# A transformer block on one core: tiles 0 to 3 of the stage between attention and MLP made one sequence

## The chip, the core and the metric

The kernel runs on one NeuronCore of a Trainium2 chip. The core's engines work from instruction queues of their own: TensorE (PE, with its weight loads as PEld), VectorE (DVE), ScalarE (ACT), GpSimd (POOL), and SyncE (SP), which here only issues DMAs. The metric is the device time of one execution in microseconds; lower is better.

## What is computed

One block for a sequence of 1024 rows of width 1024, in float32. The reference, cut to what matters:

```python
def _hybrid_mixer(h, ...):            # two attentions side by side, 8 heads of 64 each
    ...
    return o @ w_out                  # o: [1024, 1024]

def _memory_xattn(h, mem, ...):       # 4 heads of 128 over a memory of 256 rows
    q = _rms_norm((h @ w_xq).reshape(B, L, 4, 128), xq_norm_g)
    ...
    s = jnp.einsum('bqhd,bmhd->bhqm', q, k) * 128 ** -0.5
    p = jax.nn.softmax(s, axis=-1)
    o = jnp.einsum('bhqm,bmhd->bqhd', p, v)
    return o.reshape(B, L, 512) @ w_xo

def _sq_relu_mlp(h, w_ff_in, w_ff_out):
    return jnp.square(jax.nn.relu(h @ w_ff_in)) @ w_ff_out

x = x + _hybrid_mixer(_rms_norm(x, norm1_g), ...)
x = x + _memory_xattn(_rms_norm(x, norm2_g), mem, ...)
x = x + _sq_relu_mlp(_rms_norm(x, norm3_g), w_ff_in, w_ff_out)
```

## The kernel before

The 1024 rows are eight tiles of 128. The program has a head (norm and input projections), a long middle part, and a tail (tiles 4 to 7 through what is left). In the middle part two streams of Python generators are woven into one program by `together` (L122): `attend`, the two attentions tile by tile, and `fill` (L1548), everything that comes after attention for tiles whose attention is done. `fill` yields an amount of work after each step, or a pair (tile, pace): it goes on when attention has finished that tile, and then gets its share of the program according to the pace. The framework's scheduler then puts the instructions of each engine in order with a timeline of its own, inserts the semaphores, and hands out buffers from rings. So the program's order is a priority, and what stands on an engine in the end has to be read from the instruction order.

Names in the profile: psS, psPT and psPV are attention's PSUM banks (scores, transposes, values). psD (two banks) and psM (one) belong to `fill`. `oT_dr` (`o` in the profile) is attention's output, written to DRAM by `finish` (L845 and L846: `oc`, then `o`). `finish` and the queries' loads (L696, `qin`) go over the SP queue like all of `fill`'s weights.

The stage around the change is `between` (L1055), called for tiles 0 and 1 and then for tiles 2 and 3. For each pair it does the following.

- Output projection of the first tile. The tile's `o` is loaded into the buffer `xl`, its rows of x into a ring of four residual buffers `b` (tag `b4`). `gemm` (L385) goes over four chunks of 256 columns of w_out; each chunk comes in four DMAs of 256 KB, into two rings of four buffers that are called `whi` and `wlo` here for their names elsewhere (`load_whole`, L310). w_out is read whole for every tile. In the profile these matmuls are `psD<-wlo,xl` and `psD<-whi,xl`; each chunk is added to the residual rows by DVE (L1048).
- Once attention has finished the second tile: its projection, in turns with the norm of the first tile (`norm_T2`, L353: square and sum on ACT, power on POOL, scaling on DVE, four transposes at a time on PE as `psM<-c_ident,relu`, copies to `xh`). Then the norm of the second tile.
- The memory attention of both tiles: w_xq (`psD<-wlo,xh`), for each tile and half of the heads the items of `memory_item` (L1150: norm of the query, transposes, scores as `psD<-h`, softmax), and when all four items are made, `memory_values` (L1185: transposes of the probabilities, L1194, then values, again `psD<-h`). The result goes to a `b` buffer.
- Output projection of the memory attention with w_xo (`psD<-wlo,b`, `psD<-whi,b`), added to the residual rows.

The residual rows of tiles 0 and 1 are then stored to DRAM (L1227). For the second pair the w_xo projection runs in turns with `pre_norms` (L1229), which loads tile 0's rows again (L1235) and tile 1's in halves (L1241, into the weight ring `wraw`) and makes the MLP's norms of these two tiles. `mlp` (L1255) loads tile 1's rows once more (L1260), makes the norms of tiles 2 and 3 and runs the MLP of all four tiles, interleaved with attention's later tiles.

## Time and profile before

| what | value |
|---|---|
| time, median of 3 runs (lowest, highest) | 1674.51 us (1671.83, 1677.1) |
| the profiled execution: time, span of its instructions | 1675.6 us, 1673.7 us |
| mean granted TensorE clock | 0.995 |
| first matmul of tile 0's output projection | 377.58 us |
| the MLP's first matmul | 613.5 us |
| DMA | 223.88 MB, mean 134 GB/s |

The span runs from the first to the last instruction of one profiled execution. An engine is busy while one of its compute instructions runs. Idle time is given with the instruction that it precedes, and with the one whose end released it. The granted clock is the share of full speed that PE was given. Attention and `fill` share PE from 378 us to the MLP; the MLP's stage runs from 613 us to its last stores at 1143 us.

### The profile page before, as it was taken

Reading aid. Unit: us, or ns where it says so; the run is one execution under the profiler, and the core shown is the slowest. Engines: PE = TensorE matmul, PEld = TensorE weight load, DVE = VectorE, ACT = ScalarE, POOL = GpSimd, SP = SyncE. Lnnn points to the kernel's source line nnn. Section 1 sums busy time; section 2 is a strip of 40 time slices with the busy share of each in tenths; the row PEclk is TensorE's granted clock in tenths of the full one; section 3 lists DMA queues with packets and bytes.
Section 4 is the critical chain, followed back from the end, with each engine's and each line's share of the span. In section 5 each row is a group of like instructions: output and inputs, shape, how many; then the busy total and the mean of one; then the engine's idle time right before and its main releaser. Section 6 shows DMA issues by size and latency. Waiting matters only on the chain.

```text
span 1673.7 us, 28995 instructions
## 1 busy us (share of the span) xinstructions
PE 1603.5 (96%) x9554; PEld 1410.7 (84%) x9554; DVE 1122.1 (67%) x2587; ACT 1112.0 (66%) x2783; POOL 960.2 (57%) x1110
## 2 busy tenths in 40 slices
PE   7998998989999889999999999999998999999998
PEld 6998997868788778888888888888888997878787
DVE  5476778776866874575565665556668657887875
ACT  5455898895698779956898559983555554444443
POOL 2265577574632547677666767672246854555466
PEclk9999999999999999999999999999999999999999
DMA  8875534348366322222222212254267452323254
GB/s 273 297 260 164 160 110 133 121 125 280 107 195 207 98 67 73 70 70 71 70 77 67 77 59 83 68 178 134 87 219 257 148 150 89 104 90 102 96 167 148
DMA packets 185447, 223.88 MB, mean 134 GB/s; under 512 B 24785, under 2 KB 138321, under 8 KB 185297
## 3 DMA queue, kind: packets, MB, share of 16 engines
q1 hardware_dynamic: 177360, 211.53, 39.6%
q0 software_dynamic: 7936, 10.49, 2.4%
q8 instruction: 76, 1.25, 0.3%
q14 instruction: 75, 0.61, 0.1%
HBM read 188.68 MB, written 33.29 MB: 133 GB/s over the span
## 4 chain that ended last, share of the span: by engine, by line
PE 64%; DVE 12%; DMA 8%; ACT 6%; POOL 5%; issue 4%; SPq 1%; ACTq 0%; POOLq 0%; DVEq 0%
PE psD L234 32%; PE psS L234 11%; PE psM L234 6%; PE psPT L234 4%; PE psPV L234 4%; PE psPT L832 4%; DVE wlo L268 2%; POOL wlo L268 2%; DMA wraw<-in_w_in_dram 2%; DVE S L815 1%; DVE pl L255 1%; DMA wraw<-in_w_ff_out_dram 1%; ACT dmask L776 1%; POOL S L822 1%; ACT whi L263 1%
## 5 line engine op out<-in xcount | busy, mean ns | idle before, releaser
L268 POOL TENSOR_TENSOR wlo<-wraw,whi 128x512 fp32r<-128x512 f32 (+1 forms) x228 | 317.0, 1396 | 197.3 <-ACT whi L263 194.6
L263 ACT ACTIVATE whi<-wraw 128x512 fp32r<-128x512 f32 x329 | 201.0, 626 | 174.2 <-DMA wraw<-in_w_ff_in_dram 30.6
L255 DVE TENSOR_TENSOR pl<-psPT,ph 128x512 fp32r<-128x512 f32 (+1 forms) x232 | 142.5, 621 | 73.9 <-ACT ph L254 72.6
L817 ACT ACTIVATE S<-S,mn 128x128 f32<-128x128 f32 (+7 forms) x192 | 143.1, 746 | 58.5 <-DVE mn L815 57.9
L234 PE MATMUL psD<-whi,h 128*128 128x512 f32 x512 | 175.8, 398 | 1.6 <-POOL h L1364 0.7
L822 POOL TENSOR_SCALAR S<-S,sums,gi 128x640 f32<-128x640 f32 (+7 forms) x128 | 111.5, 880 | 104.7 <-DVE sums L820 87.5
L254 ACT ACTIVATE ph<-psPT 128x512 fp32r<-128x512 f32 (+1 forms) x232 | 122.7, 541 | 49.7 <-PE psPT L832 42.0
L832 PE MATMUL psPT<-c_ident,S 128*128 128x128 f32 x816 | 132.5, 274 | 6.2 <-POOL S L822 4.0
L234 PE MATMUL psD<-wlo,xh 128*128 128x256 f32 (+1 forms) x512 | 131.3, 310 | 1.5 <-POOL wlo L268 0.8
L234 PE MATMUL psD<-whi,xh 128*128 128x256 f32 (+1 forms) x512 | 129.9, 312 | 2.7 <-DMA whi<-W 1.9
L268 DVE TENSOR_TENSOR wlo<-wraw,whi 128x512 fp32r<-128x512 f32 (+2 forms) x101 | 97.7, 975 | 51.0 <-ACT whi L263 48.1
L234 PE MATMUL psD<-whi,xl 128*128 128x256 f32 (+1 forms) x432 | 120.4, 315 | 0.2
L234 PE MATMUL psS<-K,qh 128*128 128x384 f32 (+3 forms) x288 | 106.7, 374 | 6.7 <-DVE mn L815 5.5
L832 PEld LDWEIGHTS psPT<-c_ident,S 128*128 128x128 f32 x816 | 97.6, 140 | 17.4 <-POOL S L822 7.7
L234 PEld LDWEIGHTS psD<-whi,h 128*128 128x128 f32 x512 | 95.6, 188 | 19.7 <-DVE b L1048 1.8
L234 PE MATMUL psD<-xh,whi 128*128 128x512 f32 (+1 forms) x296 | 102.7, 347 | 0.0
L234 PE MATMUL psD<-xh,wlo 128*128 128x512 f32 (+1 forms) x296 | 102.0, 345 | 0.0
L234 PE MATMUL psD<-xl,whi 128*128 128x512 f32 (+1 forms) x296 | 102.0, 346 | 0.0
L234 PE MATMUL psD<-wlo,h 128*128 128x512 f32 x256 | 101.3, 397 | 0.3 <-POOL wlo L268 0.3
L234 PEld LDWEIGHTS psD<-whi,xh 128*128 128x128 f32 x512 | 91.8, 191 | 7.4 <-issue 1.6
L234 PE MATMUL psS<-K,ql 128*128 128x384 f32 (+3 forms) x288 | 96.3, 338 | 0.4 <-DVE ql L255 0.4
L234 PEld LDWEIGHTS psD<-wlo,xh 128*128 128x128 f32 x512 | 91.6, 191 | 5.3 <-POOL wlo L268 1.2
(406 smaller groups left out, 5112.6 us busy)
## 6 DMA issues: line engine op xcount, KB each, us to landing
wraw<-in_w_ff_in_dram SPq DMA_DIRECT2D x44, 512.0 KB, 3.8
wraw<-in_w_ff_in_dram SPq DMA_DIRECT2D x64, 256.0 KB, 2.7
wraw<-in_w_ff_out_dram SPq DMA_DIRECT2D x64, 256.0 KB, 2.6
wraw<-in_w_ff_out_dram SPq DMA_DIRECT2D x24, 512.0 KB, 4.6
w<-in_w_ff_out_dram SPq DMA_DIRECT2D x20, 512.0 KB, 5.9
wlo<-in_w_out_dram SPq DMA_DIRECT2D x36, 256.0 KB, 5.1
whi<-in_w_out_dram SPq DMA_DIRECT2D x36, 256.0 KB, 5.1
wraw<-in_w_in_dram SPq DMA_DIRECT2D x24, 256.0 KB, 5.2
```

What stands on the lines that cost most here:

```text
L234: te.matmul(o, a, b, start=start, stop=stop)
L254: late["round"] = s.activation(hi, src, AF.Copy).ins
L255: late["split"] = v.tensor_tensor(lo, src, hi, op=ALU.subtract).ins
L263: s.activation(hi, raw, AF.Copy)
L268: (v if l == "v" else g).tensor_tensor(lo, raw, hi, op=ALU.subtract)
L776: s.activation(mask, src, AF.Sign, bias=c, accum_out=over)
L815: v.tensor_tensor_reduce(out=dst, in0=sp, in1=m, scale=1.0, scalar=mn[:, 0:1] if i else 3e38, op0=ALU.add, op1=ALU.min, accum_out=low)
L817: s.activation(S, S, AF.Exp, bias=low, scale=-1.0, accum_out=sums[:, hh:hh + 1])
L822: g.tensor_scalar(Ss[hh], Ss[hh], sums[:, hh:hh + 1], 1.0 if gate is None else gate[:, hh:hh + 1], op0=ALU.mult, op1=ALU.mult)
L832: te.transpose(p2[:, j, hh, :], S[:, (c + j) * P:(c + j + 1) * P], ident)
```

## The change

The two calls of `between` for tiles 0 to 3 become one generator, `four_tiles`. In its program order:

- Projection of tile 0; after attention's tile 1, the projection of tile 1 in turns with tile 0's norm; tile 1's norm; the first pair's memory scores and values.
- After attention's tile 2: **tile 2's output projection**, and only then the first pair's w_xo projection. Before, w_xo came first.
- After attention's tile 3: tile 3's projection in turns with tile 2's norm, tile 3's norm, the second pair's memory attention, and its w_xo projection in turns with the MLP's norms of tiles 0 and 1.

All four tiles' residual rows stay in the four `b` buffers until the MLP. The two stores and the reloads are gone, and the norm of tile 1 is an ordinary one. One buffer `xl` of four rows' width (`room`) holds two tiles' `o` in turns, the first pair's memory result and the norm's gain, which is loaded once instead of twice. The second pair's memory result lies in two buffers of the ring `h`. `between` keeps only its use for tiles 4 to 7, whose work is the same; its inner functions for the memory attention move to `heads`.

```diff
+    def four_tiles(pool, x2, made):
+        four = [[(c * 256, 256)] for c in range(4)]
+        room = pool.tile([P, 4, DM], F32, tag="xl", name="xl")
+        _, xf, xt_of = xT(pool, 4, True)
+        gb2 = [room[:, 3, c * 512:(c + 1) * 512] for c in range(2)]
...
+        def begin(t):
+            o = room[:, t % 2].rearrange("p (k n) -> p k n", n=P)
+            for c in (1, 0):
+                nc.sync.dma_start(o[:, c * 4:c * 4 + 4, :], oT_dr[t][c])
+            if t == 0:
+                for u in range(2):
+                    x2[u] = ring(pool, "b4", [P, DM])
+                    nc.sync.dma_start(x2[u], I["x"][0, u * P:(u + 1) * P, :])
+                nc.sync.dma_start(room[:, 3], row(W["norm2_g"]).to_broadcast([P, DM]))
+            elif t > 1:
+                x2[t] = ring(pool, "b4", [P, DM])
+                nc.sync.dma_start(x2[t], I["x"][0, t * P:(t + 1) * P, :])
+            return [lambda _, k: o[:, k, :]]
...
+        def rows_out(t, first=None):
+            yield from gemm(pool, begin(t), 8, 1, W["w_out"], four, add(t), first, None, LAST_FIRST)
...
+        first = [list(weights(pool, [None], 8, W["w_out"], four[0], None, LAST_FIRST))]
+        yield from rows_out(0, first)
+        yield 1, PACES[1]
+        yield from alternate(rows_out(1), normed(0))
+        yield from normed(1)
+        yield from memory_heads(0)
+        yield 2, PACES[2]
+        yield from rows_out(2)
+        yield from made.pop(("xo", 0))
+        yield 3, PACES[2]
+        yield from alternate(rows_out(3), normed(2))
+        yield from normed(3)
+        yield from memory_heads(2)
+        yield from alternate(made.pop(("xo", 2)), pre_norms(pool, made, x2))
...
     def pre_norms(pool, made, x2s):
         made["x"] = xT(pool, 4)
         made["g"] = gain2(pool, W["norm3_g"])
-        x2s[0] = ring(pool, "b4", [P, DM])
-        nc.sync.dma_start(x2s[0], x2_dr[0])
-        norm_T2(pool, x2s[0], made["g"], xt_of(0))
...
+        for t in range(2):
+            yield from norm_of(pool, x2s[t], made["g"], made["x"][2](t))
...
-        yield from between(dn, 0, 2, {}, False, pace=PACES[1])
-        yield 2, PACES[2]
         x2s, made = {}, {}
-        yield from between(dn, 2, 2, x2s, True, None, lambda: pre_norms(dn, made, x2s), pace=PACES[2])
+        yield from four_tiles(dn, x2s, made)
```

Three places in the instruction order show what moves.

The SP queue at the start of tile 0, from the second pair of w_out loads on, before (`o_96` and `o_95` are tile 0's attention output, `in_x` the residual rows):

```order
L314 DMA wlo<-in_w_out_dram 128x2x256
L314 DMA whi<-in_w_out_dram 128x2x256
L1086 DMA b_5876<-in_x_dram 128x1024
L1086 DMA b_5877<-in_x_dram 128x1024
L1093 DMA xl<-o_96 128x512
L1093 DMA xl<-o_95 128x512
L314 DMA wlo<-in_w_out_dram 128x2x256
```

The attention output stood behind the rows of tiles 0 and 1. The same place now:

```order
L314 DMA wlo<-in_w_out_dram 128x2x256
L314 DMA whi<-in_w_out_dram 128x2x256
L1217 DMA xl<-o_96 128x512
L1217 DMA xl<-o_95 128x512
L1221 DMA b_5879<-in_x_dram 128x1024
L1221 DMA b_5881<-in_x_dram 128x1024
L1222 DMA xl<-in_norm_g_dram 128x1024
L314 DMA wlo<-in_w_out_dram 128x2x256
```

It now stands ahead of them, and the gain (`in_norm_g`) has moved up. The SP queue now, further on, after twelve of tile 0's sixteen w_out loads:

```order
L314 DMA whi<-in_w_out_dram 128x2x256
L696 DMA qin<-q_83 128x256
L1225 DMA b_6965<-in_x_dram 128x1024
L696 DMA qin<-q_84 128x256
L1225 DMA b_7612<-in_x_dram 128x1024
L273 DMA wraw<-in_w_ff_in_dram 128x2x256 x2
L314 DMA wlo<-in_w_out_dram 128x2x256
```

The rows of tiles 2 and 3 and two loads of the MLP's first weights, which stood in the second pair's stage and behind it, have moved here.

PE at the end of the first pair's memory attention, before (`h` memory scores and values, L1194 the transposes of probabilities, `wlo,b` the w_xo projection, psS, psPT and psPV attention):

```order
L234 MATMUL psD<-h 128x256 x2
L234 MATMUL psD<-wlo,b_6517 128x256 x2
L234 MATMUL psPV<-ph,V_129 128x256
L1194 MATMUL psM<-c_ident,relu 128x128 x4
L234 MATMUL psD<-h 128x256 x4
L234 MATMUL psS<-K,qh 128x512 x2
L234 MATMUL psPV<-pl,V_129 128x256
```

and now (`wlo,xl` and `whi,xl` are tile 2's output projection here):

```order
L234 MATMUL psD<-h 128x256 x2
L234 MATMUL psD<-wlo,xl 128x256 x2
L234 MATMUL psD<-whi,xl 128x256 x2
L234 MATMUL psD<-wlo,xl 128x256 x2
L234 MATMUL psD<-whi,xl 128x256 x2
L234 MATMUL psPV<-pl,V_129 128x256
L234 MATMUL psPV<-ph,V_129 128x256
L234 MATMUL psPV<-pl,V_129 128x256
L832 MATMUL psPT<-c_ident,S 128x128 x3
L1125 MATMUL psM<-c_ident,relu 128x128 x4
```

Eight matmuls of tile 2's projection stand where two of the w_xo projection stood; the w_xo projection follows behind tile 2's.

PE between the second pair's w_xo projection and the MLP, from the third to the fourth norm transposes there, before:

```order
L334 MATMUL psM<-c_ident,relu 128x128 x4
L234 MATMUL psPV<-ph,V_128 128x256
L234 MATMUL psS<-K,qh 128x384
L234 MATMUL psS<-K,ql 128x384
L234 MATMUL psS<-K,qh 128x256
L234 MATMUL psS<-K,ql 128x256
L234 MATMUL psPV<-pl,V_128 128x256
L234 MATMUL psS<-K,qh 128x384
L234 MATMUL psS<-K,ql 128x384
L334 MATMUL psM<-c_ident,relu 128x128 x4
```

and now:

```order
L334 MATMUL psM<-c_ident,relu 128x128 x4
L234 MATMUL psS<-K,qh 128x384
L234 MATMUL psS<-K,ql 128x384
L234 MATMUL psPV<-pl,V_129 128x256
L234 MATMUL psS<-K,qh 128x256
L234 MATMUL psS<-K,ql 128x256
L234 MATMUL psS<-K,qh 128x384
L832 MATMUL psPT<-c_ident,S 128x128 x2
L234 MATMUL psS<-K,ql 128x384
L832 MATMUL psPT<-c_ident,S 128x128 x6
L334 MATMUL psM<-c_ident,relu 128x128 x4
```

Fifteen attention matmuls stand there instead of eight. From the last matmul of the w_xo projection to the MLP's first one there are 65 attention matmuls, where there were 44. Elsewhere the order of all engines shifts too, to the end of the program, as the scheduler's timeline is another.

More of the change, by code (lines that the diff above doesn't have):

```diff
@@ L1122, in between, with heads @@
+    def heads(pool, nt, xo_of):
         kx, pts, items, prs = {}, {}, [], {}
[L1123 to L1126 removed]
         def consume_q(ci, t, pt):
@@ L1221, in between @@
         last = (row_by_row if "res" in late else gemm)(pool, by_tile, 4, nt, W["w_xo"], four, add_to)
-        yield from alternate(last, then()) if then else last
+        yield from last
         for t in range(nt):
@@ L1565, in fill @@
                 dn.tile([P, 2, 8, 256], F32, tag="xl", name="xl"), rows[:, 1, :].rearrange("p (k n) -> p k n", k=8)]
-        yield from between(dn, 4, 2, late["x2s"], False, None, None, room)
+        yield from between(dn, 4, 2, late["x2s"], False, None, room)
     rest = fill()
```

154 lines of the change are left out of this document (60 added, 94 removed).

## The prediction

> **What bounds the kernel now.** I read the page first, for the share of each engine over the whole span.
>
> ```profile
> span 1673.7 us, 28995 instructions
> PE 1603.5 (96%) x9554; PEld 1410.7 (84%) x9554; DVE 1122.1 (67%) x2587; ACT 1112.0 (66%) x2783; POOL 960.2 (57%) x1110
> ```
>
> PE is busy for 1603.5 of 1673.7 us, so 70 us of PE idle is all that a new order can win without taking work from PE; the change takes none. The next view is the table of stretches, over the four stages of the program: head, tiles 0 to 3 up to the MLP, MLP, tail. Its columns: length, then busy time (count) of PE, weight loads, DVE, ACT, POOL, then granted clock, DMA share, GB/s.
>
> ```profile
> 0.00:360.00 360.00, 331.44 (x2480) 312.40 (x2481) 247.45 (x744) 252.14 (x823) 198.54 (x296) 0.99 0.57 182
> 360.00:620.00 260.00, 241.62 (x1426) 210.87 (x1425) 190.17 (x535) 198.05 (x534) 122.47 (x179) 1.00 0.53 164
> 620.00:1236.00 616.00, 609.88 (x3335) 526.02 (x3334) 365.59 (x869) 456.92 (x1044) 386.60 (x400) 1.00 0.28 86
> 1236.00:1673.70 437.70, 420.56 (x2320) 361.42 (x2318) 318.87 (x441) 204.85 (x384) 252.55 (x236) 0.99 0.45 143
> ```
>
> The stage that the change rewrites is 360 to 620: 260.0 - 241.6 = 18.4 us of PE idle. The MLP behind it has 6.1 us in 616, so whatever attention work is shifted there is as good as hidden. The same table in stretches of 20 us shows where the 18.4 us lie.
>
> ```profile
> 360.00:380.00 20.00, 14.76 (x87) 11.71 (x87) 14.70 (x43) 19.55 (x62) 14.13 (x24) 1.00 0.71 224
> 380.00:400.00 20.00, 19.80 (x110) 17.44 (x109) 14.54 (x39) 13.35 (x40) 9.51 (x11) 1.00 0.98 314
> 440.00:460.00 20.00, 16.93 (x111) 13.81 (x109) 19.43 (x57) 17.79 (x53) 15.49 (x25) 1.00 0.22 61
> 460.00:480.00 20.00, 19.30 (x120) 16.88 (x121) 14.72 (x38) 19.45 (x54) 9.76 (x16) 1.00 0.53 164
> 480.00:500.00 20.00, 19.98 (x117) 18.13 (x115) 10.55 (x30) 18.19 (x53) 6.18 (x11) 1.00 0.67 216
> 500.00:520.00 20.00, 19.62 (x104) 16.75 (x104) 11.32 (x31) 18.51 (x49) 3.98 (x5) 1.00 0.95 298
> 540.00:560.00 20.00, 18.43 (x117) 16.54 (x115) 17.12 (x60) 11.31 (x34) 7.61 (x10) 1.00 0.35 109
> 560.00:580.00 20.00, 17.01 (x109) 13.86 (x109) 16.48 (x48) 16.18 (x42) 14.04 (x24) 1.00 0.44 116
> 600.00:620.00 20.00, 15.95 (x102) 13.40 (x100) 16.86 (x41) 15.70 (x34) 6.53 (x8) 1.00 0.17 54
> ```
>
> Four places: before the first projection (5.24 us), the first pair's memory scores (3.07 + 0.70), the second pair's (1.57 + 2.99), and the norms before the MLP (4.05). Where projections run (380 to 400, 480 to 520) PE is full, and DMA nearly so.
>
> **The change part by part.** *Start of tile 0.* PE's timeline (start, length, instruction, in brackets the idle time before it and who ended it):
>
> ```profile
> 373.09 0.63 PE L722 MATMUL psPT<-c_ident,qd 128*128 128x128 f32 x4 [1.70 <-DVE pl L255]
> 375.99 0.56 PE L234 MATMUL psS<-K,iql 128*128 128x384 f32 x2 [0.66 <-DVE iql L255]
> 376.72 0.33 PE L832 MATMUL psPT<-c_ident,S 128*128 128x128 f32 x1 [0.17 <-POOL S L822]
> 377.58 1.13 PE L234 MATMUL psD<-wlo,xl 128*128 128x256 f32 x4 [0.53 <-DMA xl<-o]
> 380.76 1.03 PE L234 MATMUL psD<-wlo,xl 128*128 128x256 f32 x4
> 381.63 1.03 PE L234 MATMUL psD<-whi,xl 128*128 128x256 f32 x4
> ```
>
> The first projection waits for the attention output `xl<-o`, and 1.70 + 0.66 + 0.17 + 0.53 = 3.06 us of idle lie in the 6 us before it. As the SP queue's rows in the section on the change show, `xl<-o` now goes ahead of the two residual tiles (2 x 0.52 MB, 3 us at some 350 GB/s, below). In PE's new order the first eight projection matmuls stand ahead of a run of 26 attention matmuls; at (381.63 - 380.76) / 4 = 0.216 us each they can fill 8 x 0.216 = 1.7 us. I take -1.5, bounds 0 to -3.1.
>
> *Extra data in front of the weights.* Each tile reads the whole of w_out, 16 loads, for 64 matmuls of 0.216 us: 4.19 MB in 13.8 us, 304 GB/s. The group of these loads between 360 and 440 us (count, size, median us to landing), and two short stretches:
>
> ```profile
> wlo<-in_w_out_dram SPq DMA_DIRECT2D x16, 256.0 KB, 4.7
> 372.00:376.00 4.00, 2.13 (x15) 1.66 (x15) 3.95 (x10) 3.90 (x12) 2.83 (x7) 1.00 0.95 351
> 396.00:400.00 4.00, 4.00 (x22) 3.52 (x21) 3.97 (x7) 0.81 (x2) 3.49 (x5) 1.00 0.77 229
> ```
>
> Here the rest of the SP queue counts. By its new order, tiles 2 and 3's residual rows (2 x 0.52 MB) and the MLP's first two weight pieces (2 x 0.26 MB), issued one by one in later stages until now, stand before w_out's last quarter for tile 0, since their buffers are free at once. 1.57 MB at 351 GB/s is 4.5 us, and all later weights of tiles 0 and 1, attention's queries (`qin`) and its output stores are queued behind them. What hides it: attention, which the new PE order puts between those projection matmuls; while PE had attention nearly alone it was busy 14.76 of 20 us, so a quarter to a third of 4.5 us is lost, +1.5. Bounds 0 (from 396 on DMA has a quarter free and catches up) and +4.5 (no attention ready).
>
> *Tile 2's projection behind the first pair's scores.* PE's idle there:
>
> ```profile
> 446.54 0.88 PE L832 MATMUL psPT<-c_ident,S 128*128 128x128 f32 x6 [0.23 <-POOL S L822]
> 449.88 0.39 PE L234 MATMUL psPV<-pl,V 128*128 128x256 f32 x1 [0.70 <-DVE pl L255]
> 453.69 0.50 PE L234 MATMUL psS<-K,qh 128*128 128x512 f32 x1 [0.36 <-DVE mn L815]
> 457.02 0.63 PE L1194 MATMUL psM<-c_ident,relu 128*128 128x128 f32 x4 [0.58 <-DVE h L255]
> 460.20 0.39 PE L234 MATMUL psPV<-pl,V 128*128 128x256 f32 x1 [1.11 <-DVE pl L255]
> 464.63 0.38 PE L234 MATMUL psPV<-pl,V 128*128 128x256 f32 x1 [0.32 <-DVE pl L255]
> 472.08 1.13 PE L234 MATMUL psD<-whi,b 128*128 128x256 f32 x4 [0.18 <-ACT b L1209]
> ```
>
> They add up to 3.48 us. By the order of PE in the section on the change, eight projection matmuls now stand before the last transposes of memory probabilities, where two stood. But none stands among the scores themselves, although nothing in their data holds them back (they share the two psD banks with scores and values, and come later in the program): the first comes with the values, so only the last three waits, 1.11 + 0.32 + 0.18 = 1.6 us, get cover. I take -1.6, bounds 0 and -3.5.
>
> *Second stretch of projections.* Gone from the queue there are the stores of tiles 0 and 1's residual rows, one reload of tile 1 and, moved ahead, tile 3's rows: 4 x 0.52 = 2.1 MB. PE idle there (480 to 520) is 0.02 + 0.38 us: -0.4, bounds 0 and -0.4. The two later reloads end no wait of PE: those below come from DVE, so their removal is worth nothing. The removed half-wise norm of tile 1, the stores' issue slots on SP and the second gain load cost no PE time either; the instructions on ACT, DVE and POOL stay within a dozen.
>
> *Norms before the MLP.*
>
> ```profile
> 604.77 0.44 PE L234 MATMUL psS<-K,iqh 128*128 128x384 f32 x1 [0.63 <-DVE mn L815]
> 610.22 0.44 PE L234 MATMUL psS<-K,qh 128*128 128x384 f32 x1 [1.93 <-DVE mn L815]
> 611.18 0.63 PE L334 MATMUL psM<-c_ident,relu 128*128 128x128 f32 x4 [0.34 <-DVE xl L255]
> 615.16 0.39 PE L234 MATMUL psS<-K,qh 128*128 128x256 f32 x1 [0.95 <-DVE mn L815]
> 615.86 0.63 PE L334 MATMUL psM<-c_ident,relu 128*128 128x128 f32 x4 [0.20 <-DVE xl L255]
> ```
>
> Between the second pair's last projection and the MLP, PE has norm transposes and attention alone. From the third to the fourth of these transposes the new order has 15 attention matmuls for 8; over the whole stretch I count 65 for 44. At 4.05 / 44 = 0.09 us of idle each, 21 more cost +1.9; if the chain of norms, not the count, sets it, 0. I take +1.0.
>
> **Sum:** -1.5 + 1.5 - 1.6 - 0.4 + 1.0 = -1.0 us. The profiled execution took 1675.6 us (span 1673.7 and 1.9 around it), 1.1 above the median of 1674.5. So 1675.6 - 1.0 - 1.1 = **1673.5**, no change that can be told: 0.3% is 5 us, about what a measurement of this kernel can tell from none.
>
> **The rivals.** *Faster, chance 0.32:* PE's busy time hides gaps inside the stream of short attention matmuls, and filling these is worth more than the idle shows. The weight loads beside the matmuls take 18.13 us in a full stretch (480 to 500), but 13.81 and 16.88 in the two of the scores: (18.13 - 13.81 + 18.13 - 16.88) x 20 / 18.13 = 6.1 us lost there, where the idle says 3.8. With that, the whole gap at the start filled and the extra data hidden: -3.1 - 6.1 - 0.4 + 0 + 1.0 = -8.6, 1665.9. The Trainium skill speaks for this measure: Perfetto Trace Analysis, section Identifying the Most-Contended Engine, holds matmul busy share for no good measure, because pipelined matmuls look smaller in the trace, and reads weight-load busy share instead; by it the scores' term alone would be up to -6.1. Against it: attention's short matmuls wait for their own chains on ACT and DVE, a projection beside them doesn't make those shorter, and PE's order has projections behind the scores only at their end.
>
> *Slower, chance 0.16:* the extra data becomes one gap on PE. The queue is issued in order, so with 1.57 MB ahead of the last quarter of tile 0's weights PE may stand for the whole 4.5 us. It decides by the length of one gap; the tail shows what a gap of 4.88 us does to the granted clock (0.82, 0.50, 0.83), while 1.93 us left it at 1.00:
>
> ```profile
> 1275.26 0.58 PE L234 MATMUL psS<-wlo,b 128*128 128x256 f32 x1 [4.88 <-DVE wlo L268]
> 1272.00:1276.00 4.00, 0.74 (x3) 0.74 (x4) 4.00 (x4) 1.06 (x3) 4.00 (x3) 0.82 0.79 251
> 1276.00:1280.00 4.00, 4.00 (x21) 4.00 (x20) 1.49 (x2) 0.60 (x1) 0.34 (x1) 0.50 0.67 213
> 1280.00:1284.00 4.00, 4.00 (x31) 4.00 (x31) 3.29 (x6) 3.22 (x7) 1.68 (x2) 0.83 0.57 187
> ```
>
> Lost clock: 4 x (0.50 + 0.17) = 2.7 us of work after the gap. In all 4.5 + 2.7 in place of 1.5: -1.0 + 5.7 = +4.7, and with no gain at the start (+1.5) +6.2: 1680.7. Against: attention stands in between, and the whole queue has to fall behind at once.
>
> The Trainium skill has a rule for this clock (TensorE: Matmul & The Clock Gate, Part 1): an idle window of about 3.4 us halves it. The 0.50 behind 4.88 us agrees; by that rule a gap of 3.4 us would decide, and no row here lies between 1.93 and 4.88.
>
> *The tail's gap, chance 0.10:* the instructions behind the MLP are ordered anew too, though their code is the same. If that 4.88 us gap goes, with its clock, -7.6 beside -1.0: 1665.9; if a second one comes, 1681.1. Half each.
>
> **How the numbers follow.** Forecast 0.42; faster 0.32 + 0.05 = 0.37, slower 0.16 + 0.05 = 0.21, within 0.3% 0.42. The range reaches from just below the faster cases (1665.9) to just above the slower ones (1681.1): 1664 to 1682.
>
> **What would show it.** Right: first projection matmul some 3 us earlier against the attention beside it; DMA full at 396 to 400 too, where it has 0.77 now; idle in the scores' stretch near 2 us; no PE gap over 2 us. Wrong: a gap over 3 us with a clock under 1.00 in the first projections, or PE idle from there to the MLP's start well below 18.4 us.

## The result and the profile after

| | before | after |
|---|---|---|
| median of the runs, on the same chip | 1675.8 us | 1693.64 us (4 runs, 1689.64 to 1696.21) |
| ratio | | 1.0103 [1.0078, 1.0129] |
| ratio of a second measurement (a2, below) | | 1.0097 [1.0078, 1.0116] |
| profiled execution, span, mean granted clock | 1675.6, 1673.7 us, 0.995 | 1692.08, 1690.3 us, 0.989 |
| first matmul of tile 0's projection | 377.58 us | 378.34 us |
| the MLP's first matmul | 613.47 us | 628.29 us |

The change costs 1.0%, some 17 us (17.8 here, 15.4 in the second), and the forecast of 1673.5 (1664 to 1682) missed it: it also lies 12 us above the slowest of the prediction's rivals (1681.1). The page of after:

```profile
span 1690.3 us, 28977 instructions
PE 1610.2 (95%) x9554; PEld 1417.0 (84%) x9554; DVE 1124.5 (67%) x2586; ACT 1109.1 (66%) x2781; POOL 961.7 (57%) x1110
```

PE has the same 9554 matmuls and is busy 6.7 us longer, at a mean granted clock of 0.989 for 0.995; no other engine has more instructions. The four stages, with the limits put where the MLP begins and ends here (columns as in the prediction):

```profile
0.00:360.00 360.00, 329.53 (x2469) 311.69 (x2470) 247.22 (x742) 251.28 (x819) 197.97 (x294) 0.99 0.57 181
360.00:634.00 274.00, 251.10 (x1481) 221.44 (x1481) 203.04 (x560) 208.02 (x566) 126.15 (x184) 0.98 0.47 145
634.00:1244.00 610.00, 603.73 (x3279) 518.46 (x3277) 356.09 (x844) 443.30 (x1014) 386.34 (x396) 1.00 0.28 87
1244.00:1690.30 446.30, 425.88 (x2328) 365.43 (x2328) 318.12 (x442) 206.52 (x385) 251.25 (x236) 0.98 0.44 140
```

PE idle is 22.9 us in the changed stage (18.4 before) and 20.4 in the tail, whose code the change doesn't touch (17.1 before); both now have a clock of 0.98. Where in the stage, in stretches of 20 us:

```profile
360.00:380.00 20.00, 14.32 (x89) 11.73 (x88) 13.33 (x41) 19.51 (x62) 13.79 (x22) 1.00 0.72 219
380.00:400.00 20.00, 19.31 (x111) 16.74 (x109) 14.97 (x43) 14.69 (x45) 9.31 (x15) 1.00 1.06 362
440.00:460.00 20.00, 16.92 (x107) 13.66 (x105) 18.13 (x54) 15.88 (x49) 11.82 (x19) 0.99 0.39 109
460.00:480.00 20.00, 17.64 (x106) 16.52 (x107) 15.27 (x34) 17.34 (x46) 12.71 (x20) 0.84 0.28 84
480.00:500.00 20.00, 20.00 (x114) 18.06 (x114) 10.41 (x25) 19.39 (x54) 4.45 (x7) 1.00 0.74 230
520.00:540.00 20.00, 18.19 (x103) 16.31 (x102) 10.91 (x31) 18.35 (x53) 7.07 (x11) 1.00 0.65 201
600.00:620.00 20.00, 17.83 (x103) 15.70 (x101) 17.50 (x40) 14.06 (x32) 6.64 (x7) 0.91 0.15 44
620.00:640.00 20.00, 17.09 (x99) 14.40 (x98) 11.32 (x33) 19.31 (x49) 8.30 (x10) 1.00 0.06 15
```

The start has not improved (5.68 us idle, 5.24 before), the scores have got worse (3.08 + 2.36, with a clock of 0.84), and the norms before the MLP too (2.17 + 2.91, and 0.91). PE's timeline names the waits that are new, two of them far behind the stage:

```profile
378.34 1.13 PE L234 MATMUL psD<-wlo,xl 128*128 128x256 f32 x4 [2.15 <-DMA xl<-o]
462.19 0.58 PE L234 MATMUL psPV<-cph,Vc 128*128 128x256 f32 x1 [4.10 <-DVE cph L895]
522.05 1.13 PE L234 MATMUL psD<-wlo,xl 128*128 128x256 f32 x4 [1.81 <-DMA xl<-o]
1286.63 1.12 PE L334 MATMUL psPT<-c_ident,relu 128*128 128x128 f32 x4 [3.72 <-DVE relu L360]
1351.27 0.74 PE L234 MATMUL psS<-h 128*128 128x256 f32 x4 [2.32 <-DVE h L255]
```

To set stages against each other I use one sum, the **loss**: PE's idle time, and its busy time times (1 - granted clock), added up over stretches of 2 us. What is left, busy time at full clock, is 1592 to 1598 us in all twenty profiles of this study (1595.9 before, 1596.3 after). So the work is the same everywhere to within 6 us, and a larger difference in time is a difference in loss. The limits are the same for every kernel, though the same work comes later in a slower one. The times are those of the profiled executions and, behind them, the medians. The medians come from six measurements, in which the kernel before took 1675.8 to 1678.0 us, so kernels are better compared by the ratios below:

| kernel | profiled | median | 0-360 | 360-634 | 634-1230 | 1230-1430 | 1430-end | sum |
|---|---|---|---|---|---|---|---|---|
| before | 1675.6 | 1675.8 | 33.2 | **18.4** | 5.4 | **12.4** | 8.4 | 77.8 |
| after | 1692.1 | 1693.6 | 33.6 | **26.6** | 4.4 | **16.6** | 12.7 | 94.0 |
| after again | 1692.5 | 1693.4 | 32.2 | **29.2** | 5.1 | **18.3** | 9.0 | 93.8 |
| e4 | 1673.7 | 1674.6 | 31.4 | 19.7 | 6.8 | 9.9 | 8.8 | 76.6 |
| e8 | 1679.0 | 1677.0 | 32.3 | 20.5 | 5.8 | 13.2 | 9.5 | 81.3 |
| e9 | 1684.5 | 1683.8 | 34.5 | 21.8 | 5.0 | 15.7 | 9.4 | 86.5 |
| e1 | 1685.0 | 1683.8 | 34.6 | 25.7 | 6.7 | 9.9 | 10.1 | 87.0 |
| e14 | 1680.2 | 1681.9 | 32.6 | 28.0 | 6.1 | 9.1 | 9.2 | 85.0 |
| e15 | 1685.5 | 1676.4 | 35.2 | 25.8 | 6.2 | 11.6 | 10.2 | 88.9 |
| e17 | 1703.8 | 1702.0 | 37.2 | 30.3 | 5.0 | 24.9 | 9.5 | 107 |

The first column warns of the scatter: up to 360 us the order of the instructions is the same, and it still ranges from 28.6 to 37.2 over the twenty profiles. A profile can also lie off its kernel's median, by 9 us for e15. A row shows where, the median with its interval shows how much.

### The profile page after: what moved, and what is told of

It reads as the page before. It is cut to its first block, busy times and chain, and to the rows that moved or that the text cites. A ratio compares the mean times of both kernels' runs of the same rounds, so it can differ in the third digit from the quotient of the medians.

```text
span 1690.3 us, 28977 instructions
## 1 busy us (share of the span) xinstructions
PE 1610.2 (95%) x9554; PEld 1417.0 (84%) x9554; DVE 1124.5 (67%) x2586; ACT 1109.1 (66%) x2781; POOL 961.7 (57%) x1110
## 4 chain that ended last, share of the span: by engine, by line
PE 47%; DVE 10%; ACT 10%; POOL 4%; issue 4%; DMA 2%; SPq 0%; POOLq 0%; ACTq 0%; DVEq 0%
PE psD L234 20%; PE psS L234 10%; PE psM L234 5%; PE psPT L234 5%; PE psPV L234 3%; ACT dmask L776 2%; PE psPT L832 2%; POOL wlo L268 2%; DVE wlo L268 1%; DMA wraw<-in_w_ff_out_dram 1%; ACT S L817 1%; ACT whi L263 1%; DVE pl L255 1%; ACT ph L254 1%; DVE isc L750 1%
## 5 line engine op out<-in xcount | busy, mean ns | idle before, releaser
L234 PE MATMUL psD<-whi,h 128*128 128x512 f32 (+1 forms) x544 | 187.4, 401 | 2.7 <-POOL h L1375 0.8
L234 PE MATMUL psD<-whi,xl 128*128 128x256 f32 (+1 forms) x464 | 128.9, 321 | 0.0
L234 PEld LDWEIGHTS psD<-whi,h 128*128 128x128 f32 x544 | 102.2, 190 | 22.2 <-POOL h L1375 1.2
L234 PE MATMUL psD<-wlo,h 128*128 128x512 f32 (+1 forms) x288 | 110.0, 398 | 1.7 <-POOL wlo L268 1.4
```

The lines of the kernel that those rows point to most:

```text
L234: te.matmul(o, a, b, start=start, stop=stop)
```

## The experiments

First theory, after the result (the expectations call it the order theory): the 4.10 us gap at 462, with the clock behind it, costs some 7 us up to the MLP, and the gaps at 1286 and 1351, which belong to the order into which the scheduler falls, some 7 us more. Rival (the parts theory): an intended part of the change costs by itself, be it tile 2's projection ahead of w_xo, the rows kept on chip or the waits at the start. The first batch undoes one part of the change at a time.

**e1**: w_xo of the first pair ahead of tile 2's projection again.

```diff
         yield from memory_heads(0)
+        yield from made.pop(("xo", 0))
         yield 2, PACES[2]
         yield from rows_out(2)
-        yield from made.pop(("xo", 0))
```

> The changed kernel with the first pair's w_xo projection put back ahead of tile 2's output projection; all else as changed. In the instruction order DVE's four top-k steps still stand ahead of cph, and the order behind the MLP is that of the kernel before. Order theory (the loss is a 4.1 us gap of PE before the matmul on cph, with the halved clock behind it, some 7 us by the MLP's start, and some 7 us of another order in the tail): the gap and its clock stay, the MLP starts at about 628, the tail's 7 us come back: 1686 (1683 to 1688). Parts theory (tile 2's projection ahead of w_xo is itself what costs): 1678 or less, the MLP's first matmul at 621 or earlier.

1683.82 us, 1.0037 [1.0019, 1.0055]: 10 us of the 17 are gone, but not where the edit is. The 4.10 us gap stands as in after (463.98), the MLP begins at 629.43, and the stage loses 25.7. Gone is the loss of the tail, 9.9 for 16.6: its PE order is that of the kernel before from 1267 us on (the last 2190 matmuls). So the gap does not come from tile 2's place, and the order theory's forecast holds here.

**e2**: the top-k's steps of the fifth tile on DVE held behind `cph`, which PE waits for at 462.

```diff
+        with tc.issue_after(st["cph"]) if t == 4 else ExitStack():
+            v.tensor_tensor(acc[:, t * P:Wd], acc[:, t * P:Wd], causal[:, 384:512], op=ALU.subtract)
+            v.tensor_scalar(sgn, bits[:, :, 1], 0.0, -1.0, op0=ALU.is_lt, op1=ALU.mult)
...
-            v.tensor_tensor(ph[64:128], p2[64:128], ph[64:128], op=ALU.subtract)
+            st["cph"] = v.tensor_tensor(ph[64:128], p2[64:128], ph[64:128], op=ALU.subtract).ins
```

> The changed kernel with the four DVE steps that prepare the top-k of tile 4's index mask (isc, dmask, tkh, tkl) held behind the cph instruction that PE waited 4.10 us for; all that the change intends is kept. The order behind the MLP comes out as in the kernel before. Order theory: no PE gap over 1.5 us at that place, clock 1.00 from 456 to 470, the MLP's first matmul at 621 to 622 instead of 628.3, and the tail's 7 us back: 1679 (1676 to 1682). Parts theory (the moved projection, the residual rows on chip or the waits for xl<-o are what costs): nothing of them is undone, so 1690 or more.

1687.16, 1.0060 [1.0038, 1.0082]. The gap is gone, the time is not: the MLP begins at 627.24, PE now waits 3.49 us for `xl<-o`, and the clock falls elsewhere. The miss refutes the first half of the order theory: that gap is not what decides the stage's length. The tail has the order of before again.

**e3**: the residual rows ahead of the attention output again, in `begin`.

```diff
-            for c in (1, 0):
-                nc.sync.dma_start(o[:, c * 4:c * 4 + 4, :], oT_dr[t][c])
             if t == 0:
                 for u in range(2):
                     x2[u] = ring(pool, "b4", [P, DM])
                     nc.sync.dma_start(x2[u], I["x"][0, u * P:(u + 1) * P, :])
+            for c in (1, 0):
+                nc.sync.dma_start(o[:, c * 4:c * 4 + 4, :], oT_dr[t][c])
...
```

> The changed kernel with the residual rows of tiles 0 and 1 loaded ahead of tile 0's attention output, as before; all else as changed. The four top-k steps still stand ahead of cph, the order behind the MLP is that of the kernel before. Order theory: the gap and its clock stay, the tail's 7 us come back: 1686 (1683 to 1688). If the first projection's place in the SP queue is worth what was predicted, the first projection matmul comes 1 to 3 us later than 378.3 and the time is 1687 to 1688. Parts theory: 1690 or more.

1685.49, 1.0054 [1.0035, 1.0074]; the first projection begins at 382.06 for 378.34. So the order that the change chose there is the better one; the tail has the order of before here too.

**e4 and e4b**: the same edit alone, in the kernel before: tile 0's `o` loaded ahead of the rows.

```diff
+        if pace:
+            for c in (1, 0):
+                nc.sync.dma_start(o_of[0][:, c * 4:c * 4 + 4, :], oT_dr[t0][c])
...
-            for c in (1, 0):
+            for c in (1, 0) if t else ():
```

> The kernel before with one edit of the change alone: tile 0's attention output loaded ahead of the residual rows of tiles 0 and 1. DVE's order keeps cph ahead of tkh and tkl, the tail's order is that of before. By the predicted term of -1.5 us: first projection matmul at 374.5 to 376.5 instead of 377.6, and 1674 beside 1675.5. If that wait isn't set by the queue but by attention's own output: the first projection stays within 0.5 us of 377.6 and the time within 1 us of before. A rival on the order alone (any edit that shifts the order costs some us at random): over 1680.

> The kernel before with the attention output ahead of the residual rows of tiles 0 and 1, once more, beside the other three: 1674 to 1676, 0.998 to 1.000 of before.

1674.57, 0.9988 [0.9969, 1.0006], and again 1676.32, 0.9994 [0.9974, 1.0013]. The first projection begins at 373.12, 8.6 us behind the store of `o` (364.51); before it was 11.95 us behind it (365.63 to 377.58), and in after 11.2 (367.17 to 378.34). The edit does in the old kernel what it doesn't do in the new one. What takes it away there is seen at the DMAs: POOL loads the memory's keys, `h<-KX`, 4 x 256 KB. The issues in the timeline of after:

```profile
369.58 2.22 POOL L1078 DMA_DIRECT2D h<-KX  x4
371.53 0.98 SPq L1217 DMA_DIRECT2D xl<-o  x2
```

The key loads in the timeline of before, and then those of e4 behind its first projection:

```profile
377.37 2.24 POOL L1147 DMA_DIRECT2D h<-KX  x4
```

```profile
373.12 2.07 PE L234 MATMUL psD<-wlo,xl 128*128 128x256 f32 x4 [0.52 <-DMA xl<-o]
376.23 2.24 POOL L1150 DMA_DIRECT2D h<-KX  x4
```

The view of DMA issues has in its last column the us from issue to landing, for after and then for e4:

```profile
xl<-o SPq DMA_DIRECT2D x2, 256.0 KB, 6.7
```

```profile
xl<-o SPq DMA_DIRECT2D x2, 256.0 KB, 4.3
```

In after the keys go out 2 us ahead of `xl<-o` and 7.8 us earlier than before, and `xl<-o` takes 6.7 us for 4.3. They land in ring `h`, in which the norm's gain had two buffers until now; the change put the gain elsewhere. Three kernels test that.

**e5**: the gain in ring `h` again.

```diff
-        gb2 = [room[:, 3, c * 512:(c + 1) * 512] for c in range(2)]
...
+        gain_of[0] = gain2(pool, W["norm2_g"])
...
+        gain_of[1] = gain2(pool, W["norm2_g"])
```

> The changed kernel with one part undone: the norm's gain is loaded into two buffers of the ring h again, once for each pair, not once into the buffer xl. By the instruction order POOL's four loads of the memory keys (h<-KX, 1.05 MB) go back to where they were before, behind tile 0's attention output; cph stands ahead of the top-k steps; the tail's order is that of before. Queue theory (taking the gain out of the ring h let POOL's key loads start at 369.6 instead of 377.4 and share the DMA engines with xl<-o, which took 6.7 us to land instead of 4.2): the first projection matmul comes some 8.6 us behind the second-last o store ahead of it (365 to 367) instead of 11.2, with a wait under 1 us; with the gap before cph and the tail's 8 us gone too: 1679 (1676 to 1682). Parts theory (the moved projection and the residual rows cost): 1688 or more, first projection at 378.

**e8**: the reverse, e4 with the gain moved out of the ring, into a third row of `xl`.

```diff
...
-                gb2 = gain2(pool, W["norm2_g"])
+                g2 = both[:, nt].rearrange("p k n -> p (k n)")
+                nc.sync.dma_start(g2, row(W["norm2_g"]).to_broadcast([P, DM]))
+                gb2 = [g2[:, c * 512:(c + 1) * 512] for c in range(2)]
```

> The kernel before with the attention output ahead of the residual rows (as in the experiment that has that edit alone: 1674.6, first projection 8.6 us behind the o store at 364.5) and, in addition, the norm's gain in the buffer xl instead of the ring h. POOL's four key loads move up as in the changed kernel. Queue theory: xl<-o lands in over 6 us, the first projection comes 10.5 to 12 us behind that store, and the time is 2 to 4 us above that experiment's: 1677 to 1679. If the key loads don't matter: 8.6 us and 1674 to 1676.

**e10**: after, with the key loads held by a wait behind POOL's power step of tile 0's norm.

```diff
+                with tc.issue_after(late.pop(("after", 0))) if ("after", 0) in late and ci == 0 else ExitStack():
+                    kx["k", ci] = stored(KX, ci)
...
```

> The changed kernel with POOL's first loads of the memory keys (h<-KX) held behind POOL's part of tile 0's norm; all that the change does is kept. cph stands ahead of tkh and tkl, the tail's order is that of before, 65 attention matmuls stand before the MLP. Queue theory: the first projection comes about 8.6 us behind the o store at 364 to 367, as where the gain stays in the ring h, with a wait under 1 us. With the stalls before the MLP left: 1685 (1682 to 1688). If the key loads don't matter there: a wait of 2 to 3.5 us for xl<-o as in the changed kernel.

e5 took 1687.57, 1.0056 [1.0034, 1.0078]: keys at 375.65, `xl<-o` in 4.5 us, first projection at 372.70, 8.8 us behind the store. e8 took 1676.96, 1.0004 [0.9990, 1.0017]. POOL's and PE's timeline of e8, then its DMA issues:

```profile
367.25 2.21 POOL L1152 DMA_DIRECT2D h<-KX  x4
375.73 1.13 PE L234 MATMUL psD<-wlo,xl 128*128 128x256 f32 x4 [1.89 <-DMA xl<-o]
```

```profile
xl<-o SPq DMA_DIRECT2D x3, 256.0 KB, 6.5
```

Put into the old kernel, the moved gain brings the keys forward by 9.0 us, `xl<-o` to 6.5 us, and the wait of 1.89. e10 took 1680.99, 1.0022 [1.0011, 1.0034]: keys at 399.98, tile 0's `xl<-o` in 3.7 us, first projection at 370.91 without a wait. In e11, e13 and e15, which hold the keys too, it lands in 4.9, 5.1 and 5.9 us, and PE still waits 0.80, 1.27 and 2.04 us for it, so the keys are not the only load that delays it. Counted from the store of `o`, the first projection comes 7.9 to 10.1 us later in the eight profiles with `o` first and late keys (e4, e4b, e5, e9, e10, e11, e13, e15), and 10.9 to 12.5 us later in the ten with early keys. So this side effect is shown in both directions; in time it is the 2.4 us between e4 and e8, within their intervals. The times of e5 and e10 can't tell it, since both have the tail of before too. The Trainium skill (DMA: Bandwidth & Descriptors, section Queues, rings and completion order) has each DMA engine go round between the queues that have work; the 4.3 and 6.7 us agree.

The gap at 462 is an order on DVE, in its timeline of after and then of before:

```profile
457.12 0.96 DVE L753 TENSOR_TENSOR isc<-isc,c_masks 128x128 f32<-128x128 f32 x1
458.66 0.48 DVE L758 TENSOR_SCALAR dmask<-isc 128x640 int16<-128x640 int16 x1
459.17 1.28 DVE L759 SCALAR_TENSOR_TENSOR tkh<-dmask,isc 128x640 int16<-128x640 int16 x1
460.37 1.31 DVE L760 TENSOR_TENSOR tkl<-isc,dmask 128x640 int16<-128x640 int16 x1
461.71 0.43 DVE L895 TENSOR_TENSOR cph<-psPT,cph 64x256 fp32r<-64x256 f32 x1
```

```profile
456.90 0.43 DVE L895 TENSOR_TENSOR cph<-psPT,cph 64x256 fp32r<-64x256 f32 x1
457.36 0.83 DVE L759 SCALAR_TENSOR_TENSOR tkh<-dmask,isc 128x640 int16<-128x640 int16 x1
```

Some 4 us of top-k stand ahead of the 0.43 us that PE waits for. In e2 and e10 `cph` goes first again. The gap stays in e1, e3, e12, e14, e17 and e18, with w_xo first or not, and is absent in e10, e13 and e15, where the keys are held. Early keys alone don't make it: e8 has none. e10 has the smallest stage of all kernels made from after (22.2, in an execution 5.5 us below its median); it still needs 19.2 us from the last four w_xo matmuls to the MLP. In e5 PE waits 3.53 us at 461.61 for `ph` of ACT, which stands on ACT behind a step that waits 3.37 us for the `tkl` of the same top-k: the same chain, by another door.

**e7 and e11**: the projection of tile 2 really beside the scores, in turns with them, alone and with the keys held as in e10.

```diff
-        yield from memory_heads(0)
         yield 2, PACES[2]
-        yield from rows_out(2)
+        yield from alternate(memory_heads(0), rows_out(2))
```

> The changed kernel with tile 2's output projection written in turns with the first pair's memory scores (as soon as attention's tile 2 is done), so that projection matmuls stand between the scores. The key loads stay early, the tail's order is that of before. If idle between the scores is a lack of ready work on PE: idle from 440 to 480 falls from 5.5 us to under 2, no gap over 1.5 us, and 1680 (1677 to 1683). If waiting for attention's tile 2 only moves the idle ahead of the scores, or the chains on DVE grow longer: 1685 or more, with a wait for xl<-o of over 2 us ahead of tile 2's projection.

> The changed kernel with tile 2's output projection in turns with the first pair's scores and the key loads held behind tile 0's norm; all residual rows stay on chip. If the stalls are separate: the scores' idle under 3 us, the first projection early, the tail as before: 1682 (1679 to 1685). If covering the first scores only takes the cover from later places (as the run with that edit alone showed: +2.8 us in the second pair's scores and +2.7 before the MLP): 1686 to 1689.

e7: 1690.93, 1.0084 [1.0062, 1.0105]; e11: 1687.45, 1.0064 [1.0042, 1.0086]. In e7 the idle of the scores (440 to 474) falls from 5.4 to 2.6 us, and the second pair's (536 to 590) rises from 3.8 to 7.5: the projection that covers one place is missing at the other. e11 gets waits of 2.73 and 2.57 us at 467 and 563. The rival of the prediction by which filling the scores gains more than the idle shows finds no support: both kernels have the tail of before, and still e7 is slower than e1 (1.0037), and e11 than e10 (1.0022), which leave the scores unfilled.

**a2**: after, unchanged.

> The changed kernel once more, unchanged, to see which of its stalls are its own. Order theory: 1693.6 within 2 us, the 4.10 us gap before cph again, a PE gap over 3 us between 1270 and 1300 and idle of over 2 us between 1340 and 1360 again, with clock under 1.00 behind the first; waits for xl<-o of 2 to 3.5 us ahead of the first projection. What doesn't come again belongs to that one execution.

1693.41, 1.0097 [1.0078, 1.0116], with waits of 4.03 us for `cph` at 463, 1.99 for `xl<-o` at 523, 4.36 and 1.87 in the tail. The gaps belong to the order; a dip of the clock at 1632 us that after had did not come again.

The next kernels go for the second pair's memory result, which the change puts into two of ring `h`'s buffers.

**e9**: e4 with that alone.

```diff
-            xo = [ring(pool, "b4", [P, 4, nt * P])]
+            xo = [ring(pool, "h", [P, 2, nt * P]) for _ in range(2)] if keep and pace else [ring(pool, "b4", [P, 4, nt * P])]
...
```

> The kernel before with the attention output ahead of the residual rows (that edit alone: 1674.6) and one more part of the change: the second pair's memory result in two buffers of the ring h instead of a residual buffer. Stores, reloads, the order of w_xo and tile 2's projection stay as before. In the instruction order 65 instead of 44 attention matmuls now stand between the last w_xo matmul and the MLP, and from before the MLP to the end PE's order is word for word that of the changed kernel. Ring theory (two buffers fewer in h hold back the load of the MLP norms' gain, so the norms of tiles 0 and 1 start late; the rest of the program then gets the changed kernel's order, with its own stalls in the tail): last w_xo matmul to the MLP's first one 18 to 20 us instead of 12.2, the tail (1230 to the end) 6 to 9 us of stall and lost clock over before's, 1685 (1681 to 1689). Interleave theory (tile 2's projection and the rows on chip are what costs): 1673 to 1677.

**e14**: after with that result in two buffers of the ring `wraw`, **e13** the same and the keys held, **e15** e13 and w_xo of the first pair ahead of tile 2's projection.

```diff
-                xs = [ring(pool, "h", [P, 2, 2 * P]) for _ in range(2)]
+                xs = [ring(pool, "wraw", [P, 2, 2 * P]) for _ in range(2)]
```

> The changed kernel with one edit: the second pair's memory result in the ring wraw instead of the ring h. Key loads stay early, the top-k steps stay ahead of cph. Ring theory: last w_xo matmul to the MLP 12 to 14 us instead of 19.5, tail's order and stalls as before; the wait for xl<-o of 2 to 3.5 us and the 4.1 us gap before cph stay: 1683 (1680 to 1686), so 8 to 13 us of the change's loss come from this one choice of buffer. If the ring is not the cause inside the change: 1688 or more.

> The changed kernel with both side effects taken away: POOL's key loads held behind tile 0's norm, and the second pair's memory result in the two buffers of the ring wraw (free there, as the MLP's first weight pieces then load later), not in the ring h. Rows on chip and tile 2's projection ahead of w_xo stay. cph ahead of tkh and tkl, tail's order as before. If the two intended parts are worth what was predicted for them (-1.6 -0.4): last w_xo matmul to the MLP 12 to 14 us, 1672 to 1675 beside a before of 1676. If the moved projection itself costs: 1678 to 1681, with the extra stall between 500 and 600.

> As the run with keys held and the result in wraw, and the first pair's w_xo projection ahead of tile 2's output projection as before. What is left of the change: all residual rows on chip, the attention output ahead of the rows at the start, one gain load less. If rows on chip cost nothing and gain nothing, only the start's gain is left: the same as the kernel before with that edit alone, 1674 to 1676, and below the run with tile 2's projection first if that order costs. If keeping the rows on chip costs in itself: 1679 or more.

**e12**: after with the rows of tiles 0 and 1 stored and loaded again (the reloads in `pre_norms` and `mlp` as before), and the result in a `b` buffer.

```diff
-                xs = [ring(pool, "h", [P, 2, 2 * P]) for _ in range(2)]
+                xb = ring(pool, "b4", [P, 4, 2 * P])
...
         yield from made.pop(("xo", 0))
+        for t in range(2):
+            nc.sync.dma_start(x2_dr[t], x2.pop(t))
...
```

> The changed kernel with the residual rows of tiles 0 and 1 stored to DRAM and loaded again as before (with the MLP's norms of these tiles as before), so that the second pair's memory result is in a residual buffer and not in the ring h; tile 2's projection still ahead of w_xo. 50 attention matmuls instead of 65 stand before the MLP. Ring theory: last w_xo matmul to the MLP 13 to 14 us, stall and lost clock there (590 to 634) 4 to 5 us instead of 6.9; the stalls at the start and before cph stay; tail as before: 1682 (1679 to 1685). Interleave theory: 1687 or more.

The way to the MLP is taken from the start of the last four w_xo matmuls to the MLP's first matmul, with the attention matmuls on PE behind the last w_xo matmul:

| kernel | median, ratio | way to the MLP | attention matmuls |
|---|---|---|---|
| before, e4 | (above) | 12.2 and 13.2 us | 44 |
| after | (above) | 19.5 us | 65 |
| e9 | 1683.76, 1.0034 [1.0021, 1.0047] | 19.6 us | 65 |
| e14 | 1681.85, 1.0027 [1.0011, 1.0043] | 17.0 us | 58 |
| e13 | 1681.60, 1.0018 [1.0001, 1.0035] | 17.9 us | 58 |
| e15 | 1676.39, 0.9998 [0.9978, 1.0018] | 17.0 us | 55 |
| e12 | 1682.93, 1.0034 [1.0022, 1.0047] | 15.5 us | 50 |

e9 is the clearest of the study. One choice of a buffer takes e4 from 0.9988 [0.9969, 1.0006] to 1.0034, gives 65 attention matmuls behind the last w_xo instead of 44, and an order of PE from the MLP's first matmul to the end that is that of after (all 5641 matmuls). With the order come the tail's gaps, in PE's timeline of e9:

```profile
1281.00 0.71 PE L334 MATMUL psPT<-c_ident,relu 128*128 128x128 f32 x4 [3.73 <-DVE relu L360]
1344.63 0.74 PE L234 MATMUL psS<-h 128*128 128x256 f32 x4 [2.58 <-DVE h L255]
```

The table of stretches, 200 us of the tail, in after and e9, which share the order:

```profile
1230.00:1430.00 200.00, 187.29 (x1211) 168.78 (x1211) 129.05 (x198) 106.37 (x213) 113.34 (x116) 0.97 0.55 172
```

```profile
1230.00:1430.00 200.00, 188.36 (x1203) 169.34 (x1203) 130.85 (x199) 103.85 (x204) 112.97 (x111) 0.97 0.55 174
```

and in e14 and before, which share the other:

```profile
1230.00:1430.00 200.00, 192.64 (x1247) 173.89 (x1246) 137.13 (x210) 109.66 (x217) 119.28 (x120) 0.99 0.56 179
```

```profile
1230.00:1430.00 200.00, 190.55 (x1205) 171.51 (x1204) 136.60 (x204) 103.50 (x204) 115.61 (x111) 0.98 0.57 182
```

By these rows PE is idle 12.7 and 11.6 us at a clock of 0.97 with the one order, and 7.4 and 9.5 us at 0.99 and 0.98 with the other. (The counts of matmuls say nothing here, as the same 200 us cut each kernel at another place.) The other way round, e14 takes the same choice out of after and wins 12 us of the 17 while its stage stays as dear (28.0, the 4.10 us gap in place); its tail has the order of before and loses 9.1. Near its place the choice moves the load of the MLP's norm gain, in SP's and PE's timeline of after and then of before:

```profile
582.40 1.02 PE L234 MATMUL psD<-wlo,h 128*128 128x256 f32 x4
585.04 0.91 SPq L428 DMA_DIRECT2D h<-in_norm_g_dram  x2
```

```profile
573.69 0.92 SPq L428 DMA_DIRECT2D h<-in_norm_g_dram  x2
574.24 1.03 PE L234 MATMUL psD<-wlo,b 128*128 128x256 f32 x4
```

Before, the gain was asked for 0.6 us ahead of the first w_xo matmul; with two of the ring's buffers held it comes 2.6 us behind it, and the norms follow it. I took these 3.2 us for what stretches the way to the MLP, and the other traces speak against it. In e13 the gain is asked for 4.8 us ahead of the first w_xo matmul and the way still takes 17.9 us, where I had expected 12 to 14; in e12 it comes 2.8 us behind and the way takes 15.5. What the way does follow, in the table above, is the number of attention matmuls that stand in it. That is work moved ahead of the MLP, and most of it is no loss: from 590 to 634 the loss grows by 2.9 us, not by 7.

Nor is the ring the whole cause of the tail's order: e1, e2, e3, e5, e7, e10 and e11 keep the result in `h`, and each has the tail of before. The order with the gaps is one into which the scheduler falls from after's and e9's state, and any of these edits takes it out. So the last question is how much an order of the tail is worth by itself.

**e17** and **e18**: after, with an edit of the tail's code alone: the two halves of the attention output of tiles 6 and 7 loaded in the other order (PE's order is after's up to about 1253 us), and the tail's norms in the opposite order of tiles.

```diff
-                for c in (1, 0):
+                for c in (0, 1):
```

```diff
-        for t in range(nt):
+        for t in reversed(range(nt)):
             yield from norm_of(pool, x2[t], gb2, xt_of(t))
```

> The changed kernel with one neutral edit in the tail alone: the two halves of the attention outputs of tiles 6 and 7 are loaded in the other order. PE's order is that of the changed kernel up to 1253 us and another from there. Tail theory (the order that the scheduler falls into behind the MLP costs about 7 us, whatever stands in the tiles' stage): MLP's first matmul at 628 to 629 as in the changed kernel, no PE gap <-DVE relu of over 3 us at 1280 to 1290, stall and lost clock from 1230 to 1430 near 10 us instead of 16.6 and 18.3: 1686 (1683 to 1689). Carried-over theory: 1692 to 1695.

> The changed kernel with the norms ahead of the memory attention of tiles 4 and 5, and of 6 and 7, made in the other order (second tile first). PE's order is that of the changed kernel up to the norms of tiles 4 and 5, near 1200 us. Tail theory: as for the run with the halves, 1686 (1683 to 1689), with other gaps in the tail; carried-over theory: 1692 to 1695.

1702.03, 1.0146 [1.0118, 1.0174], and 1694.80, 1.0101 [1.0074, 1.0128]. Neither wins anything: e18 is where the carried-over theory of its expectation put it, and e17 misses the numbers of both theories, on the far side. Its waits in the tail, in PE's timeline:

```profile
1294.72 1.12 PE L334 MATMUL psPT<-c_ident,relu 128*128 128x128 f32 x4 [4.25 <-DVE relu L360]
1364.56 0.80 PE L234 MATMUL psS<-h 128*128 128x256 f32 x2 [5.90 <-ACT h L254]
```

Its tail loses 24.9 us. Over all kernels the same 200 us of the tail cost between 9.1 and 24.9 us, by order alone for all that these traces show: 9.1 to 13.2 in the fifteen profiles that have before's order from 1270 us on at the latest, 15.7 to 18.3 in after, its repeat, e9 and e18. Before's order has a gap of its own, for `psS<-wlo,b` (4.88 us in before, 3.32 to 5.16 in the fifteen); in after's order it is gone, and the two at 1286 and 1351 stand in its place.

No kernel of the study beats the one before beyond its interval; e4, its one good edit alone, comes closest.

## Why the prediction was wrong

The loss of about 17 us is 8 to 11 in the stage (26.6 and 29.2 for 18.4), about 5 in the tail (16.6 and 18.3 for 12.4), and the rest behind it and within the scatter. The forecast had -1.0 for the stage and nothing for the tail, and three steps failed above all: the gain load that was put at nothing, the cover that tile 2's projection was to give, and the tail that was to stay as it was. Step by step:

- **Start, -1.5.** Right by itself: e4 has the first projection 3.3 us sooner behind the store of `o`, and is 1 to 2 us faster in the medians, though not beyond its intervals. Wrong in the new kernel, because of the step "the second gain load cost no PE time either". Taking it out of ring `h` freed two buffers for POOL's key loads, 1.05 MB that go out ahead of `xl<-o`. I had followed SP's queue and not POOL's. Gained: nothing (378.34 for 377.58).
- **Extra data, +1.5.** The DMA is full at 396 to 400, as said (share 1.05, 0.77 before), and PE idle from 386 to 440, summed over its timeline, went from 0.2 to 0.6 us: +0.4, near the lower bound. The rival of the slower side, one gap of 4.5 us there, did not occur.
- **Tile 2's projection behind the scores, -1.6.** This step failed outright. Idle from 440 to 474 went from 3.8 to 5.4 us, and 2.1 us of clock came on top: +3.7. Two things were wrong. The cover itself is worth nothing: where the gap at 462 is absent and tile 2 goes first, that stretch still has 3.8 (e10) and 3.6 us of idle (e13), and 3.7 with w_xo first (e15). And I looked only at what covers PE's old waits: the order of DVE had changed too, and put 4 us of top-k ahead of `cph`. That gap is not of the placing, as e1 shows, but "no PE gap over 2 us" fell with it. In time the placing, without the side effects, is e13 against e15: 1.0018 [1.0001, 1.0035] with tile 2 first, 0.9998 [0.9978, 1.0018] with w_xo first. That is no gain and perhaps a cost.
- **The faster rival, chance 0.32.** Not borne out by e7 and e11. The fair pair is e11 and e10, which both hold the keys: 1.0064 [1.0042, 1.0086] with the scores filled, 1.0022 [1.0011, 1.0034] without.
- **Second stretch, -0.4.** Right (no idle from 480 to 520), and outweighed by a new wait of 1.81 us for `xl<-o` at 522.
- **Norms before the MLP, +1.0.** Right in sign, and the 65 matmuls were counted rightly; 590 to 634 cost 1.3 us more idle and 1.6 of clock, +2.9. The same 1.6 of clock are lost there in e4 and e4b, which have 44 of these matmuls as before, so they may not be the change's. Of the 4.05 us in the sum, 0.95 + 0.20 lie behind the MLP's first matmul (613.47); with 2.90 / 44 the upper bound is 1.4, not 1.9. That the second pair's result shares ring `h` with the gain of these norms was not seen.
- **Removed stores and reloads, 0.** The runs agree: e15 has them removed and stands at 0.9998 [0.9978, 1.0018], so their price is nothing to within 4 us.
- **The tail, chance 0.10.** The order of the tail did change, but neither half of the rival came as it was put. The 4.88 us gap went, which was to win 7.6, and gaps of 3.72 and 2.32 us came in its place, with a clock of 0.50 behind the first; the sum is a loss of 4.2 (5.9 in the repeat). I gave the rival a tenth, as though a new order of the tail were the exception. In this study it is not: e9, e14 and e17 move the tail's loss by 6 to 8 us each.

(One matmul at the start takes 0.87 / 4 = 0.218 us, where the prediction has 0.216; nothing hangs on it.)

What stays open: why the scheduler puts 55 to 58 attention matmuls ahead of the MLP even with ring `h` free, what besides the early keys makes the gap at 462, and what in the scheduler's state picks the tail's order.

## What to carry to other kernels

When a buffer moves, list who else draws from the ring it leaves and the ring it joins, on every queue: a freed buffer starts someone's transfer earlier, and a held one delays the next. Read the new order on the engines that feed PE, not only on PE: for each thing PE waits for, see what now stands ahead of it. Where a scheduler orders the whole program, the change of one stage draws a new order for all that follows; measure an unrelated reorder once to know how far such a draw moves the time (here up to 8 us, half a per cent), and don't credit it to the edit.

## What was not expected of the hardware

The clock fell for some 3 to 4 us behind gaps shorter than the 4.88 us known from before. The 4.10 us gap of after, in stretches of 2 us:

```profile
458.00:460.00 2.00, 0.10 (x1) 0.00 (x0) 1.97 (x5) 1.96 (x9) 2.00 (x3) 0.89 0.11 24
460.00:462.00 2.00, 0.00 (x0) 0.00 (x0) 1.97 (x3) 0.81 (x3) 2.00 (x2) 0.50 0.00 0
462.00:464.00 2.00, 1.81 (x8) 1.81 (x9) 1.74 (x5) 0.76 (x3) 2.00 (x4) 0.50 0.00 0
464.00:466.00 2.00, 2.00 (x12) 2.00 (x11) 1.70 (x5) 2.00 (x7) 1.92 (x5) 0.50 0.00 0
466.00:468.00 2.00, 2.00 (x13) 1.83 (x13) 1.41 (x3) 2.00 (x7) 0.43 (x2) 0.91 0.21 66
```

It cost 0.11 x 0.10 + 0.50 x (1.81 + 2.00) + 0.09 x 2.00 = 2.1 us of work. And e4, where PE stood 1.70 us before 371.97 and 0.52 us before 373.12:

```profile
372.00:374.00 2.00, 1.48 (x6) 1.15 (x7) 1.97 (x5) 1.97 (x7) 0.91 (x2) 0.74 1.03 341
374.00:376.00 2.00, 2.00 (x6) 1.53 (x6) 0.80 (x2) 1.90 (x6) 2.00 (x3) 0.50 0.92 355
376.00:378.00 2.00, 2.00 (x13) 1.77 (x12) 0.00 (x0) 0.71 (x4) 2.00 (x5) 0.91 1.06 359
```

Gaps of 1.70 and 0.52 us cost 0.26 x 1.48 + 0.50 x 2.00 + 0.09 x 2.00 = 1.6 us of work here, while before stood 1.70, 0.66, 0.17 and 0.53 us at the same place with the clock at 1.00, e11 1.68 and 0.80 us with 1.00 too, and e13 stood 2.35 us at 517 with 1.00 behind it. The Trainium skill (TensorE: Matmul & The Clock Gate, Part 1) has the clock halved after an idle window of about 3.4 us, and the window run freely. The 4.10 us gap agrees, the 1.70 us one does not by its length alone. Nor do the summed gaps decide, since e11 stood longer than e4 and kept its clock; that PE's activity within a window decides, and where the window happens to begin, would fit, but no run here shows it.
